# Attention quotients as small reciprocals copied out by ScalarE, gate products dealt out thinner, and two of four low parts on VectorE, in a two-layer diffusion trunk

## The chip, the core and the metric

The kernel runs on one core of a Trainium2 chip. A core has five engines with a queue of instructions each: TensorE (PE: matrix products and transposes; weight loads are shown as PEld), VectorE (DVE), ScalarE (ACT), GpSimd (POOL) and SyncE (SP, which here only issues DMA transfers). Each engine works through its queue in order and waits on semaphores for what other engines and transfers have to deliver. The metric is the device time of one execution in microseconds (us); lower is better.

## The reference

Two layers of a trunk with two attention branches side by side. 512 latent tokens on an 8 x 64 grid and 256 context tokens; model width 1024; branches A and B have 8 query heads of 64 each.

```python
for l in range(DEPTH):                       # 2 layers
    hx = rmsnorm(x) * (1 + scale_x) + shift_x      # scale, shift, gate = silu(c) @ w_ada + b_ada
    a_k, a_v, b_k, b_v, a_q, b_q, a_z, b_z, g_a, g_b = split(hx @ w_in)
    a_att = neighbourhood attention (8 x 16 window, position bias, QK-norm) plus all context keys
    qb = rope_2d(rmsnorm(b_q)); kb = rope_2d(rmsnorm(b_k))
    b_att = softmax(qb . k_all / 8) @ v_all        # 2 key/value heads, 768 keys
    o_a = (a_att * silu(a_z)) @ w_o_a
    o_b = (b_att * silu(b_z)) @ w_o_b
    merged = sigmoid(g_a) * o_a + sigmoid(g_b) * o_b
    x = x + gate_x * (merged @ w_out)              # context tokens likewise, in layer 0 only
```

All inputs and the output are fp32.

## The kernel before, in words

**Precision.** An fp32 product is made of three products of a faster format: each operand is split into a high part (a rounded copy) and a low part (the rest), and high x high, low x high and high x low are summed (lines 423 to 425). So each weight tile `raw` that is loaded needs a cast by ScalarE (`whi`, L393 or L408) and a subtraction by VectorE or GpSimd (`wlo`, L396 or L410). Softmax weights are turned by DMA: ScalarE casts `p` to fp16 (`h`, L824), VectorE or GpSimd subtracts for the low part (L825), and a DMA transpose (L829, issued by SyncE) writes `ht`.

**Stages of a layer.** Projections and the neighbourhood attention of branch A; the projection of branch B's keys and values; then the stages that the change touches:

- *Branch B's queries.* `for t in range(qt): tok_proj(w_q, 512, a_hx, t, evac_bq)` runs one tile of 128 tokens after the other (six in layer 0, four in layer 1). Per tile the evacuation squares on ScalarE, sums on VectorE (L493), takes the power on GpSimd (L496), multiplies on VectorE (L505), applies the rotary or, for context tokens, the norm weight (`rr`, L574, L579), and TensorE transposes `rr` some pieces later (L517).
- *Gate products.* In layer 0 the list `bg` holds what the adaptive gate still needs: two loads of the conditioning vector and 32 dot products on VectorE (L285), two for each 128x512 tile `rawb` of w_ada that SyncE loads into one of two buffers. Twelve items run in the key/value projection, 22 are left for the query projection, `run(bg, 4)` after each tile. In layer 1 the list is empty there.
- *Fill pieces.* Products that the attention doesn't depend on (gate columns of w_in, then the output projection of branch A, `o_chunks("a", ...)`) are cut into pieces; `PRE_GQ * len(spans)` of them (four in layer 0) run ahead of the attention, the others between its blocks. Their accumulator `psf` is one PSUM buffer, emptied by ScalarE (L612) or, for branch A's output, by VectorE (`tg`, L694).
- *Grouped-query attention.* Eight blocks u. `gq_first(u)`: four times scores on TensorE (L879, L880) into one of two PSUM buffers `pss`, the maximum on VectorE (L1151), the exponential on ScalarE (L1152), which frees `pss` and adds up the row sums `r`, then the transposition as above. `gq_second(u)`: `divide`, then the products with the values (`pair_values`, L844) and the multiplication into `zb` (L1179). `divide` (L831 to L837) takes the 128x4 sums of a block, repeats each 64 times, takes the reciprocal of the 128x256 result on VectorE (L834), turns it by two TensorE transposes (L836) and multiplies it into the gate `zb` (L837). There are 20 divisions: eight blocks in each layer, and four for context queries in layer 0 (sums `rc`).
- *`prepare`*, a fill piece: splits the gated output of branch A, `za`, into `gah` (four casts by ScalarE, L658) and `gal` (four subtractions by GpSimd, L659), and issues the first two of four gate loads `tg` (1.5 MB each in layer 0).

**What sets the order.** The kernel is written in a tile framework whose scheduler gives each engine its order of instructions from a timeline of its own; a few orders are tied by hand (`behind`). So an edit in one place moves rows in many others.

Of the kernel before, what the change touches and what calls it, by code (L numbers as in the profile page):

```python
# [12 lines left out]
ALU = mybir.AluOpType  # L13
# [38 lines left out]
def R(ap):  # L52
    return ap.bitcast(F32R)
# [7 lines left out]
def hybrid_kernel(es: ExitStack, tc, x, ctx, cvec, w_ada, w_ada0, small, gvec, w_in, w_o_a, w_o_b, w_out,  # L61
# [521 lines left out]
    def layer(l, hx, nxt, start):  # L583
        first = l == 0
        ntok = NTOK if first else NLAT
# [67 lines left out]

        def hilo(src, dst, fs, lo_eng=G, parts=((0, ntok),)):
            sv = src.rearrange("p (f n) -> p f n", f=4)
            for n0, n1 in parts:
                for f in fs:
                    S.copy(R(dst[0][:, f, n0:n1]), sv[:, f, n0:n1])  # L658
                    lo_eng.tensor_tensor(R(dst[1][:, f, n0:n1]), sv[:, f, n0:n1], dst[0][:, f, n0:n1], ALU.subtract)  # L659

# [20 lines left out]
        def prepare():  # L681

            gated["a"] = hilo_tiles("ga")
            hilo(za, gated["a"], range(4))
            for c in (0, 2):
                tg[c] = big("tg")
                load_tg(c)
# [90 lines left out]
        if True:  # L778
# [52 lines left out]
            def divide(ps, r, dst, back):  # L831

                rb = att["p"].tile([128, 2, 128], F32, tag="rb", name=nm("rb"), bufs=2)
                V.reciprocal(rb.rearrange("p i (e d) -> p i e d", e=2), r.unsqueeze(3).to_broadcast([128, 2, 2, 64]))  # L834
                for i in range(2):
                    T.transpose(ps[:, 128 * i:128 * i + 128], rb[:, i, :], ident)  # L836
                V.scalar_tensor_tensor(dst, ps, back, dst, ALU.mult, ALU.mult)  # L837
# [274 lines left out]
            for t in range(qt):  # L1112
                tok_proj(w_q, 512, a_hx, t, evac_bq)
                run(bg, 4)
                if t == STAGE_T[0]:
                    split_vb()
                if t in STAGE_T:
                    e = STAGE_T.index(t)
                    stage_k(kbv[:, 0, :], e, gkt[e][0], gkt[e][1], True)

            zb = big("zb")
            for i in range(PRE_GQ * len(spans)):
                run(fill, 1)
                turn_late(1 if i == 0 else 0)
            bp_es.close()
            gq_es = open_att(f"gq{l}", 768, NP_GQ[l], 0, NH_GQ[l])
# [64 lines left out]
        with tc.tile_pool(name=f"mrg{l}", bufs=1, reuse_waits="tile") as mp:  # L1191
# [3 lines left out]
            for v in range(nv):  # L1195
                src = gd[l][8 * v:8 * v + 8].rearrange("k p -> (k p)").unsqueeze(0)
                nc.sync.dma_start(gv[:, v, :], src.to_broadcast([128, DM]))
            hilo(zb, gated["b"], [3], V, spans)
            mg = []
# [313 lines left out]
```

## Time and profile before

| | us |
|---|---|
| three runs of the kernel | 1111.32, 1114.02, 1115.77 (median 1114.02) |
| the profiled execution | 1115.85 |
| its span, from the first instruction to the last | 1114.1 |
| TensorE busy | 1074.7 |
| VectorE, ScalarE, GpSimd busy | 783.1, 607.9, 441.2 |
| mean granted TensorE clock | 0.995 |

The profile is of one execution. Its span is the time in which instructions ran; 1.75 us of the execution's time lie around it. "Busy" counts an engine's own instructions, not its waits. A wait is put down to the instruction that released it: "PE pst L836 <- DVE rb L834: 2.2, 2, 1.4" reads: TensorE's line 836, which writes `pst`, waited for VectorE's line 834, which wrote `rb`; 2.2 us in all, 2 times, the longest 1.4. In the stretches, times count from the start of the span: 330 to 371 is the query projection of layer 0, 371 to 381 the fill pieces behind it, 381 to 540 the grouped-query attention of layer 0, 925 to 1064 that of layer 1.

### The profile page before, as it was taken

How to read it: one execution, taken by the hardware profiler on the slowest of the kernel's cores; microseconds unless marked ns; L12 is line 12 of the kernel's file. 1: busy time of each engine (PE TensorE's matmuls, PEld its weight loads, DVE VectorE, ACT ScalarE, POOL GpSimd, SP SyncE). 2: the span in 40 equal slices, each digit the busy share in tenths (PEclk: the TensorE clock that was granted, in tenths of full speed). 3: DMA queues.
4: the chain of work that ended last, by engine and by line, in shares of the span. 5: the costliest groups of instructions: out<-in, count | busy, mean ns of one | idle time of the engine just before them, and what ended most of it. 6: DMA issues, size and time to landing. Idle time of an engine off the chain costs nothing. (4 is left out here: it accounts for less than half of the span.)

```text
span 1114.1 us, 17673 instructions
## 1 busy us (share of the span) xinstructions
PE 1074.7 (96%) x6032; PEld 883.2 (79%) x6032; DVE 783.1 (70%) x1626; ACT 607.9 (55%) x1236; POOL 441.2 (40%) x375
## 2 busy tenths in 40 slices
PE   8999999899999899988999999999999999999998
PEld 5688888788887778876888778888877888877777
DVE  4667799974388486766576875466997665879573
ACT  6464279776333467665231275444999346676430
POOL 1054235554256143353412444332455472453531
PEclk9999999999999999999999999999999999999999
DMA  9455325555545277789624532453555536889742
GB/s 369 149 169 149 90 70 116 124 137 121 174 121 179 86 177 185 174 219 248 210 76 130 189 120 69 136 170 102 126 145 126 150 113 171 195 236 218 201 151 77
DMA packets 236002, 171.83 MB, mean 154 GB/s; under 512 B 160140, under 2 KB 201864, under 8 KB 234248
## 3 DMA queue, kind: packets, MB, share of 16 engines
q1 hardware_dynamic: 228576, 156.31, 51.6%
q0 software_dynamic: 2368, 7.87, 2.1%
q10 hardware_dynamic: 4968, 6.53, 1.8%
q8 instruction: 47, 0.77, 0.3%
q14 instruction: 43, 0.35, 0.1%
HBM read 115.58 MB, written 17.32 MB: 119 GB/s over the span
## 5 line engine op out<-in xcount | busy, mean ns | idle before, releaser
L825 POOL TENSOR_TENSOR h<-p,h 128x256 f16<-128x256 f32 (+2 forms) x104 | 111.2, 1078 | 199.5 <-ACT h L824 154.2
L410 POOL TENSOR_TENSOR wlo<-raw,whi 128x512 fp32r<-128x512 f32 x70 | 97.7, 1399 | 136.8 <-ACT whi L408 100.5
L423 PE MATMUL psf<-hx,whi 128*128 128x512 f32 (+1 forms) x360 | 137.3, 382 | 1.5 <-DVE zt L614 1.2
L424 PE MATMUL psf<-hx,whi 128*128 128x512 f32 (+1 forms) x360 | 135.7, 377 | 0.0
L425 PE MATMUL psf<-hx,wlo 128*128 128x512 f32 (+1 forms) x360 | 135.3, 376 | 0.0
L408 ACT CAST whi<-raw 128x512 fp32r<-128x512 f32 x136 | 82.9, 620 | 74.0 <-DMA raw<-in_w_in_dram 52.5
L423 PE MATMUL psx<-whi,hx 128*128 128x512 f32 (+1 forms) x328 | 121.7, 373 | 0.0
L424 PE MATMUL psx<-wlo,hx 128*128 128x512 f32 (+1 forms) x328 | 120.1, 367 | 1.3 <-DVE wlo L396 1.3
L425 PE MATMUL psx<-whi,hx 128*128 128x512 f32 (+1 forms) x328 | 120.1, 367 | 0.0
L396 POOL TENSOR_TENSOR wlo<-raw,whi 128x512 fp32r<-128x512 f32 x40 | 59.2, 1483 | 126.5 <-ACT whi L393 83.1
L393 ACT CAST whi<-raw 128x512 fp32r<-128x512 f32 x88 | 54.0, 624 | 94.3 <-PE psx L425 32.1
L496 POOL TENSOR_TENSOR ss<-ss,ehalf 128x8 f32<-128x8 f32 (+2 forms) x40 | 63.6, 1594 | 78.0 <-DVE ss L493 69.6
L824 ACT CAST h<-p 128x256 f16<-128x256 f32 (+2 forms) x136 | 81.2, 617 | 12.3 <-DMA ht<-h 9.3
L1151 DVE CUSTOM_DVE_ANT_0 p<-pss,vb 128x768 f32<-128x768 f32 x64 | 59.9, 949 | 35.1 <-PE pss L880 31.2
L1152 ACT ACTIVATE p<-pss,mx 128x768 f32<-128x768 f32 x64 | 57.5, 901 | 41.0 <-DVE mx L1151 40.6
L423 PEld LDWEIGHTS psf<-hx,whi 128*128 128x128 f32 x360 | 67.8, 188 | 14.7 <-DVE zt L614 1.6
L410 DVE TENSOR_TENSOR wlo<-raw,whi 128x512 fp32r<-128x512 f32 x66 | 60.8, 925 | 26.3 <-ACT whi L408 26.2
L425 PEld LDWEIGHTS psf<-hx,wlo 128*128 128x128 f32 x360 | 67.8, 188 | 11.7
L424 PEld LDWEIGHTS psf<-hx,whi 128*128 128x128 f32 x360 | 67.9, 189 | 11.2 <-issue 0.6
L424 PEld LDWEIGHTS psx<-wlo,hx 128*128 128x128 f32 x328 | 62.0, 189 | 11.6 <-DVE wlo L396 2.4
L425 PEld LDWEIGHTS psx<-whi,hx 128*128 128x128 f32 x328 | 61.9, 189 | 10.5 <-DVE hx L339 0.4
L423 PEld LDWEIGHTS psx<-whi,hx 128*128 128x128 f32 x328 | 61.9, 189 | 9.4 <-issue 0.2
(330 smaller groups left out, 2938.9 us busy)
## 6 DMA issues: line engine op xcount, KB each, us to landing
raw<-in_w_in_dram SPq DMA_DIRECT2D x168, 256.0 KB, 3.0
rawb<-in_w_ada_dram SPq DMA_DIRECT2D x48, 256.0 KB, 2.7
raw<-in_w_out_dram SPq DMA_DIRECT2D x32, 256.0 KB, 2.9
tg<-gs SPq DMA_DIRECT2D x4, 1536.0 KB, 8.4
rawx<-in_w_ada_dram SPq DMA_DIRECT2D x4, 1024.0 KB, 10.2
rawy<-in_w_ada_dram SPq DMA_DIRECT2D x4, 1024.0 KB, 9.9
gs<-zt ACTq DMA_DIRECT2D x16, 256.0 KB, 2.6
raw<-in_w_o_a_dram SPq DMA_DIRECT2D x16, 256.0 KB, 3.7
```

Source lines behind the costliest of these rows:

```text
L393: S.copy(hi[:, :n], raw[:, :n])
L396: e.tensor_tensor(lo[:, :n], raw[:, :n], F(hi[:, :n]), ALU.subtract)
L408: S.copy(hi, raw)
L410: lo_eng(i).tensor_tensor(lo, raw, F(hi), ALU.subtract)
L423: T.matmul(ps, lhs[0], rhs[0], start=first, stop=False)
L424: T.matmul(ps, lhs[0], rhs[1], start=False, stop=False)
L425: T.matmul(ps, lhs[1], rhs[0], start=False, stop=last)
L496: G.tensor_tensor(ss, ss, ehalf[:, :n], ALU.pow)
L824: S.copy(h[:, 0], p[:, :n])
L825: eng.tensor_tensor(h[:, 1], p[:, :n], h[:, 0], ALU.subtract)
L1151: V.tensor_tensor_reduce(p, pss, lift, -1.0, 3e38, ALU.add, ALU.min, mx[:, 0:1])
L1152: S.activation(p, pss, AF.Exp, bias=mx[:, 0:1], accum_out=r[:, i, e:e + 1])
```

## The change

Three edits.

1. `divide` takes the reciprocal of the 128x4 sums in place on VectorE, and ScalarE then writes each of them 64 times side by side into `rb`.
2. After each tile of the query projection three items of `bg` run where four did, and after each of the four fill pieces one more; whatever is then left runs at once.
3. `hilo` takes a tuple of engines and goes round it: `gal` 0 and 2 on VectorE, 1 and 3 on GpSimd, in both layers. The other calls keep their engine.

```diff
-        def hilo(src, dst, fs, lo_eng=G, parts=((0, ntok),)):
+        def hilo(src, dst, fs, lo_eng=(G,), parts=((0, ntok),)):
...
-                    lo_eng.tensor_tensor(R(dst[1][:, f, n0:n1]), sv[:, f, n0:n1], dst[0][:, f, n0:n1], ALU.subtract)
+                    lo_eng[f % len(lo_eng)].tensor_tensor(R(dst[1][:, f, n0:n1]), sv[:, f, n0:n1], dst[0][:, f, n0:n1], ALU.subtract)
...
-            hilo(za, gated["a"], range(4))
+            hilo(za, gated["a"], range(4), (V, G))
...
-                V.reciprocal(rb.rearrange("p i (e d) -> p i e d", e=2), r.unsqueeze(3).to_broadcast([128, 2, 2, 64]))
+                V.reciprocal(r, r)
+                S.copy(rb.rearrange("p i (e d) -> p i e d", e=2), r.unsqueeze(3).to_broadcast([128, 2, 2, 64]))
...
             for t in range(qt):
                 tok_proj(w_q, 512, a_hx, t, evac_bq)
-                run(bg, 4)
+                run(bg, 3)
...
             for i in range(PRE_GQ * len(spans)):
                 run(fill, 1)
                 turn_late(1 if i == 0 else 0)
+                run(bg, 1)
+            run(bg, len(bg))
...
-            hilo(zb, gated["b"], [3], V, spans)
+            hilo(zb, gated["b"], [3], (V,), spans)
```

Lines behind the edits move: L836 becomes L837, L837 L838, L844 L845, L879 L880, and from the second edit on by three (L1151 becomes L1154, L1152 L1155, L1179 L1182).

VectorE's order at the end of layer 0's query projection, from the first context tile's `rr` (L574) to the second's, which is the last tile's. `junk` and `rawb` as outputs are dot products (L285; their second rows, of the sums, are left out), `wlo` a low part, `ss` the norm's sums. Before:

```order
594 L574 TENSOR_TENSOR rr_4048<-ry_4046,gbc_3413 128x512
595 L410 TENSOR_TENSOR wlo_3796<-raw_3792,whi_3794 128x512
596 L285 ISA rawb_4012,asum<-rawb_4012,cb_3888 128x512
598 L493 TENSOR_REDUCE ss_815_4091<-sq_3407 128x8
599 L285 ISA junk_4058,asum<-rawb_4056,cb_3888 128x512
601 L285 ISA rawb_4056,asum<-rawb_4056,cb_3888 128x512
603 L285 ISA junk_4063,asum<-rawb_4061,cb_3888 128x512
605 L505 TENSOR_TENSOR ry_4095<-psx_4066,ss_815_4091 128x512
606 L285 ISA rawb_4061,asum<-rawb_4061,cb_3888 128x512
608 L574 TENSOR_TENSOR rr_4097<-ry_4095,gbc_3413 128x512
```

With the change:

```order
587 L505 TENSOR_TENSOR ry_4036<-psx_4007,ss_802_4032 128x512
588 L574 TENSOR_TENSOR rr_4038<-ry_4036,gbc_3413 128x512
589 L410 TENSOR_TENSOR wlo_3796<-raw_3792,whi_3794 128x512
590 L285 ISA junk_4048,asum<-rawb_4046,cb_3888 128x512
592 L493 TENSOR_REDUCE ss_811_4080<-sq_3407 128x8
593 L285 ISA rawb_4046,asum<-rawb_4046,cb_3888 128x512
595 L285 ISA junk_4053,asum<-rawb_4051,cb_3888 128x512
597 L505 TENSOR_TENSOR ry_4084<-psx_4055,ss_811_4080 128x512
598 L574 TENSOR_TENSOR rr_4086<-ry_4084,gbc_3413 128x512
599 L285 ISA rawb_4051,asum<-rawb_4051,cb_3888 128x512
```

Between the two L574 there were five dot products and are three now; seven follow the last L574 where two did.

VectorE around `prepare` in layer 0 (`p` with `mx` is a score's maximum, the first `zb` of a pair L837 or L838 the quotient times the gate). Before:

```order
752 L1179 TENSOR_TENSOR zb_4110<-pst_5539,zb_4110 128x256
753 L834 RECIPROCAL rb_5731<-r_1068_5468 128x256
754 L834 RECIPROCAL rb_5773<-rc_5312 128x256
755 L1151 ISA p_5663,mx_5664<-pss_5658,vb_3419 128x768
757 L1151 ISA p_5676,mx_5677<-pss_5671,vb_3419 128x768
759 L837 SCALAR_TENSOR_TENSOR zb_4110<-pst_5729,vb_3419,zb_4110 128x256
760 L837 SCALAR_TENSOR_TENSOR zb_4110<-psv_5730,vb_3419,zb_4110 128x256
```

With the change:

```order
747 L834 RECIPROCAL r_1068_5474<-r_1068_5474 128x4
...
753 L1182 TENSOR_TENSOR zb_4100<-pst_5545,zb_4100 128x256
754 L1154 ISA p_5670,mx_5671<-pss_5665,vb_3419 128x768
756 L838 SCALAR_TENSOR_TENSOR zb_4100<-pst_5736,vb_3419,zb_4100 128x256
757 L834 RECIPROCAL rc_5316<-rc_5316 128x4
758 L659 TENSOR_TENSOR gal_5412<-za_1053,gah_5411 128x768 x2
759 L1154 ISA p_5683,mx_5684<-pss_5678,vb_3419 128x768
764 L838 SCALAR_TENSOR_TENSOR zb_4100<-psv_5737,vb_3419,zb_4100 128x256
```

Two reciprocals in a row stood ahead of the next block's first maximum; now two low parts stand between its first and second.

ScalarE in the last block of layer 0 with the change (L1155 exponentials, L902 those of the context, L835 the new copies):

```order
547 L1155 ACTIVATE p_5894,r_1145_5875<-pss_5889,mx_5895 128x768
548 L1155 ACTIVATE p_5907,r_1145_5875<-pss_5902,mx_5908 128x768
549 L1155 ACTIVATE p_5920,r_1145_5875<-pss_5915,mx_5921 128x768
550 L408 CAST whi_6154<-raw_6152 128x512
551 L835 COPY rb_6074<-r_1145_5875 128x256
552 L824 CAST h_5898<-p_5894 128x768
553 L658 CAST gbh_6064<-zb_4100 128x768 x3
```

The copy comes right behind the block's last exponential and one cast, ahead of three casts `h` that the transposes need.

SyncE at `prepare` in layer 0 (`tg` gate loads, `ht` and `vb` transposes). Before:

```order
232 L662 DMA tg_5415<-gs_83 128x3072
233 L662 DMA tg_5417<-gs_85 128x3072
234 L829 DMA_TRANSPOSE ht_5467<-h_5517 128x12x128
235 L829 DMA_TRANSPOSE vb_3419<-h_5535 128x8x128
236 L829 DMA_TRANSPOSE ht_5656<-h_5667 128x12x128
237 L405 DMA raw_5811<-in_w_o_a_dram 128x2x256
238 L662 DMA tg_6050<-gs_84 128x3072
239 L662 DMA tg_6052<-gs_86 128x3072
```

With the change:

```order
232 L829 DMA_TRANSPOSE ht_5473<-h_5523 128x12x128
233 L662 DMA tg_5421<-gs_83 128x3072
234 L662 DMA tg_5423<-gs_85 128x3072
235 L662 DMA tg_6060<-gs_84 128x3072
236 L829 DMA_TRANSPOSE vb_3419<-h_5541 128x8x128
237 L405 DMA raw_5820<-in_w_o_a_dram 128x2x256
238 L829 DMA_TRANSPOSE ht_5663<-h_5674 128x12x128
```

The third gate load has moved up behind the first two, ahead of the context's transpose and of the next block's first; the fourth now stands alone, three transposes later.

## The prediction

> **What bounds the kernel now.** I read the page's head first: whichever engine fills the span sets the time.
>
> ```profile
> span 1114.1 us, 17673 instructions
> PE 1074.7 (96%) x6032; PEld 883.2 (79%) x6032; DVE 783.1 (70%) x1626; ACT 607.9 (55%) x1236; POOL 441.2 (40%) x375
> ```
>
> TensorE is busy for 1074.7 of 1114.1 us. The change takes no matmul away, so all that it can win is TensorE's idle time (39 us in the whole program) and time at a halved clock. Next come the stretches that it touches, as busy time by engine (PE, PEld, DVE, ACT, POOL, then granted clock, DMA share, GB/s): the last projection of branch B in layer 0, the fill pieces behind it, the grouped-query attention of layer 0 in two parts, and that of layer 1 in two parts.
>
> ```profile
> 330.00:371.00 41.00, 36.71 (x177) 29.97 (x176) 35.65 (x76) 14.14 (x27) 22.00 (x13) 0.96 0.43 145
> 371.00:381.00 10.00, 10.00 (x57) 8.71 (x57) 0.90 (x3) 3.86 (x7) 1.29 (x1) 1.00 0.20 66
> 381.00:484.00 103.00, 100.52 (x692) 83.92 (x691) 75.31 (x131) 69.14 (x146) 33.98 (x23) 1.00 0.73 169
> 484.00:540.00 56.00, 48.70 (x340) 38.48 (x339) 35.45 (x59) 29.55 (x57) 28.47 (x20) 0.97 1.01 259
> 925.00:990.00 65.00, 63.89 (x375) 52.59 (x373) 47.20 (x71) 46.00 (x86) 26.09 (x17) 1.00 0.74 177
> 990.00:1064.00 74.00, 69.90 (x435) 54.95 (x434) 57.28 (x82) 42.35 (x76) 34.60 (x24) 1.00 0.88 224
> ```
>
> TensorE idles 4.3, 0, 2.5, 7.3, 1.1 and 4.1 us there, 19 us in all. What it waits for, in the last projection (2 rows), then in layer 0's attention (7), then in layer 1's (6):
>
> ```profile
> PE pst L517 <- DVE rr L574: 3.2, 1, 3.2
> PE pst L517 <- DVE rr L579: 1.0, 1, 1.0
> ...
> PE pst L836 <- DVE rb L834: 2.2, 2, 1.4
> PE pst L844 <- DVE zb L837: 1.7, 1, 1.7
> PE psf L424 <- POOL gal L659: 1.5, 1, 1.5
> PE psf L423 <- DVE tg L694: 1.5, 4, 0.5
> PE pss L879 <- ACT p L1152: 1.2, 3, 0.7
> PE pss L879 <- ACT p L901: 0.7, 1, 0.7
> PE pst L844 <- DMA ht<-h: 0.7, 1, 0.7
> ...
> PE pss L879 <- ACT p L1152: 2.3, 3, 1.5
> PE psf L423 <- DVE tg L694: 1.2, 3, 0.6
> PE pst L836 <- DVE rb L834: 0.8, 1, 0.8
> PE psf L423 <- ACT zt L612: 0.3, 1, 0.3
> PE psf L424 <- POOL gal L659: 0.3, 1, 0.3
> PE psf L423 <- ACT gbh L658: 0.3, 1, 0.3
> ```
>
> Nearly all of them are on VectorE, or on ScalarE behind a maximum of VectorE.
>
> **Part 1, the spread dot products.** The timeline at the end of the last projection:
>
> ```profile
> 364.59 0.69 DVE L285 CUSTOM_DVE_ANT_0 junk<-rawb,cb 128x512 bf16<-128x512 f32 x1 [1.68 <-DMA rawb<-in_w_ada_dram]
> 365.21 0.69 DVE L505 TENSOR_TENSOR ry<-psx,ss 128x512 f32<-128x512 f32 x1
> 366.42 0.69 DVE L574 TENSOR_TENSOR rr<-ry,gbc 128x512 f32<-128x512 f32 x1
> 382.12 0.96 DVE L1151 CUSTOM_DVE_ANT_0 p<-pss,vb 128x768 f32<-128x768 f32 x1 [10.16 <-PE pss L880]
> 367.25 1.08 PE L517 MATMUL pst<-ident,rr 128*128 128x128 f32 x4 [3.25 <-DVE rr L574]
> 369.41 0.63 PE L424 MATMUL psx<-hx,whi 128*128 128x512 f32 x1
> 370.35 0.40 PE L424 MATMUL psx<-hx,whi 128*128 128x512 f32 x1
> ...
> 367.00:370.00 3.00, 2.75 (x9) 2.39 (x10) 2.62 (x10) 1.58 (x4) 0.00 (x0) 0.51 0.00 0
> ```
>
> A dot product that waits 1.68 us for its weight tile stands in VectorE's line ahead of the last tile's L505 and L574, and the transposes of that tile wait 3.25 us. The windows' row at the bottom gives half clock for the 3 us after (0.63 us for a matmul that takes 0.40 once it is over): 1.5 us of lost rate, of which I count 1.3, since its first 0.25 is the stall's own. In the new order L505 and L574 stand ahead of two of these products, one load's wait sooner, and the tile before goes two products earlier. The 3.25 and the 1.3 go if L574 ends before about 364.0, where TensorE asks for it; one dot on a new load stays ahead of it, so I leave 0.5 us of wait. The 1.05 for L579, whose engine was busy with dots too, goes as well. Gain 3.25 + 1.05 + 1.3 - 0.5 = **5.1**. The five dots that move past L574, 0.69 us each, 3.5 in all, land in VectorE's pause of 10.16 us before the first maximum; TensorE runs fill pieces there with VectorE busy 0.90 of 10. Their loads move on SyncE's queue as well, ahead of the fill's fourth weight load; without that cover the first scores would wait the 3.5. Bounds: 0 (the loads hold L505 as before) to 5.6.
>
> The Trainium skill ("TensorE: Matmul & The Clock Gate", Part 1: The HAM clock gate) has the clock halved after an idle window of about 3.4 us. The 3.25 us stall and the row at 0.51 agree; by that rule the 1.3 goes with the stall, as I count it, but the second halved stretch below, behind waits of 1.40 us at most, would not be tied to one stall.
>
> **Part 2, the reciprocals.** The groups, and two small stand-ins that the kernel already has:
>
> ```profile
> L834 DVE RECIPROCAL rb<-r 128x256 f32<-128x256 f32 x16 | 28.0, 1748 | 1.0 <-ACT p L1152 0.8
> L834 DVE RECIPROCAL rb<-rc 128x256 f32<-128x256 f32 x4 | 6.9, 1723 | 0.3 <-ACT p L901 0.3
> L781 DVE RECIPROCAL r<-r 128x2 f32<-128x2 f32 x8 | 1.3, 157 | 1.5 <-ACT p L901 1.5
> L824 ACT CAST h<-p 128x256 f16<-128x256 f32 x64 | 24.1, 401 | 2.1 <-DVE p L787 1.0 <-issue 0.5
> ```
>
> VectorE gives up 28.0 + 6.9 = 34.9 us and takes on 20 x 0.157 = 3.1; ScalarE takes on 20 x 0.40 = 8.0, priced by a copy of the same width. A copy from a stride of zero is in no row: the bounds are 0.40 and the 1.75 of the reciprocal that read so, and I take 0.40, since the reciprocal's price fits its arithmetic. From a quotient that is ready to the transposes it is 0.16 + 0.40, some 0.7 with a handover between engines (an estimate), in place of 1.75: each wait on rb shrinks by about 1.0. So of 2.2 us in layer 0 (0.8 and 1.4) I take 1.8, in layer 1 all 0.8. The 1.7 for zb stands behind two reciprocals in a row; but two low parts now stand at that place (part 3), so half of it: 0.8. Of the waits for tg and for L1152 (2.7 and 3.5 us), which end when VectorE comes to an L694 or a maximum, I take a third with less in the line: 0.5 and 0.4 in layer 0, 0.4 and 0.8 in layer 1.
>
> The copy is also a new wait. ScalarE's order puts it behind the block's last exponentials, and each copy waits for VectorE's small reciprocal with casts and the next block's exponentials queued behind; those free the two score buffers for TensorE. I charge 1.5 us for it; bounds 0 (ScalarE is busy 53 to 71% in these stretches) and the rival below.
>
> **Part 3, the low parts of gal.**
>
> ```profile
> L659 POOL TENSOR_TENSOR gal<-za,gah 128x768 fp32r<-128x768 f32 x4 | 7.9, 2015 | 0.0
> L659 POOL TENSOR_TENSOR gal<-za,gah 128x512 fp32r<-128x512 f32 x4 | 5.5, 1397 | 0.0
> 518.67 0.95 DVE L825 TENSOR_TENSOR h<-p,h 128x768 f16<-128x768 f32 x1
> 539.25 3.93 DVE L659 TENSOR_TENSOR gbl<-zb,gbh 128x512 fp32r<-128x512 f32 x2
> ```
>
> Two of four leave GpSimd, so the chain of 7.9 us ends about 4 us sooner and the waits on it (1.5 and 0.3) go. On VectorE the like is 0.95 us alone, but 1.97 each for two smaller ones beside GpSimd's own; I take 2.0, so 4.0 us in one block, against 3.4 us of two reciprocals that stood there. Between 1.9 and 5: no net term.
>
> The Trainium skill ("SBUF — State Buffer", SBUF: two separate sides) says that GpSimd and a VectorE instruction with two SBUF inputs hold the shared port in turn, the loser blocked for the whole instruction. The row 539.25 looks like it. Taken whole, it makes the pair cost VectorE the 4.0 that I use.
>
> **The second half of layer 0's attention** needs a brake. DMA share is 1.01 over 484 to 540 (above): four gate loads of 1.5 MB share the queues with the transposes of h. And there is a second halved stretch:
>
> ```profile
> 527.00:530.00 3.00, 3.00 (x9) 2.11 (x7) 1.87 (x2) 1.28 (x4) 3.00 (x3) 0.50 1.21 271
> ```
>
> Where transfers set the pace, a VectorE that is ready sooner waits for them. Layer 0's candidates are 1.8 (rb) + 0.8 (zb) + 1.5 (gal) + 0.5 (tg) + 0.4 (L1152) = 5.0, and 0.7 for half of this stretch's loss: 5.7. I take half, **2.9**. Layer 1's are 0.8 (rb) + 0.3 (gal) + 0.4 + 0.8 = 2.3, with DMA at 0.74 to 0.88; I take **2.0**.
>
> **The sum.** 5.1 + 2.9 + 2.0 - 1.5 = 8.5 us from the profiled execution's 1115.85 (span 1114.1 and 1.75 around it) gives 1107.35. That execution lies at the top of the three runs, 1.8 above their median of 1114.02, so the median comes to 1105.5: **1105**, rounded down. A scheduler orders all instructions anew, past the attention too; I put that at 0, with 3 us either way.
>
> **The rivals.**
>
> *Transfers set the pace* in both second halves (DMA 1.01 and 0.88, a third gate load now stands directly behind the first two on SyncE, ahead of two transposes that it followed before). For it: the same row's share. Against: of 9.5 us waited in layer 0 only 0.7 is put down to a DMA. Then the projection gains 5.1, the two early rb waits about 0.8 each, less 1.5 for the copies: 5.2, or 1114.0 - 5.2 = 1109.
>
> *ScalarE's line is the new bound* (slower). A copy reaches the head before VectorE has come to its small reciprocal, which stands behind low parts (0.95 to 2.0 us) and a maximum (0.96): up to 3 us in which the next exponentials stand still. Speaking for it: L1152 already holds scores back 3.5 us. Against: a wait costs TensorE only once both score buffers are full, and a block has 17 to 20 us (139 and 159 us for 8 of them). At 1.0 us of TensorE for each of 20 copies, 20 less the gains of 5.1 + 2.9 + 2.0 makes 10 us lost: 1124. It is slower than before from 0.5 us each.
>
> *The projection's stall stays* because GpSimd's power and the load, not the dots, end last: 1.0 of 5.1 is won, the rest as forecast: 1114.0 - 4.4 = 1109.6.
>
> **Chances.** Forecast (1100 to 1108) 0.58; transfers 0.18; stall stays 0.12; ScalarE's line 0.07; something better than the forecast, with the halved stretch and the whole of the waits gone (up to 19 us of idle), 0.05. The range 1099 to 1114 leaves out the slower rival and the best case and takes in the bounds between; the likeliest case alone is 1100 to 1108. What differs by less than 0.5% (5.6 us) can hardly be told from no change: faster is below 1108.4, which holds the forecast, the best case and few of the others: 0.64. Slower is above 1119.6: 0.07. Same: 0.29.
>
> **What would show it.** Right: no wait on rr at L517 above 0.5 us and clock 1.00 around 367; VectorE's busy time down by about 32 less 7 for the low parts; the new copies at 0.40; no wait on gal. Wrong: the copies at over 1 us, more waiting on L1155 (L1152 before) than 3.5 us, TensorE waiting for qs or pss at the first scores because dots run late, or as much idle time in 484 to 540 with DMA in the place of VectorE.

## The result, and the profile after

The changed kernel takes 1097.99 us (median of four runs, 1095.73 to 1103.31) where the kernel before takes 1113.88: 0.9864 of it, 95% interval 0.9835 to 0.9892. Measured a second time it gave 0.9863 (0.9841 to 0.9884). That is 14 to 16 us faster, and the time lies below the predicted range, which began at 1099. The direction was right; nearly half of the gain was not foreseen.

The page's head after:

```profile
span 1095.5 us, 17697 instructions
PE 1066.4 (97%) x6032; PEld 882.3 (81%) x6032; DVE 757.7 (69%) x1630; ACT 613.6 (56%) x1256; POOL 438.5 (40%) x371
```

The same 6032 matmuls fill 8.3 us less, for the most part because fewer of them ran at half clock (the mean granted clock is 1.000 in place of 0.995, which is worth 5.6 us), and TensorE idles 29.1 us in place of 39.4. The stretches that answer to those of the prediction (query projection, fill pieces, layer 0's attention in two parts, layer 1's in two; columns as there):

```profile
330.00:367.00 37.00, 33.72 (x170) 27.67 (x169) 30.76 (x60) 12.06 (x21) 20.95 (x13) 1.00 0.50 150
367.00:378.00 11.00, 11.00 (x62) 9.57 (x61) 5.76 (x19) 3.96 (x9) 1.38 (x1) 1.00 0.29 94
378.00:475.00 97.00, 95.24 (x662) 80.86 (x661) 63.72 (x126) 70.91 (x150) 36.35 (x24) 1.00 0.74 174
475.00:529.00 54.00, 50.93 (x373) 42.08 (x372) 31.28 (x67) 32.30 (x64) 25.15 (x18) 1.00 0.99 271
914.00:975.00 61.00, 60.44 (x360) 49.80 (x359) 39.35 (x68) 46.55 (x87) 26.07 (x17) 1.00 0.78 187
975.00:1046.00 71.00, 69.24 (x439) 55.20 (x438) 48.20 (x84) 44.13 (x80) 33.84 (x22) 1.00 0.90 229
```

The clock is 1.00 in all of them: both halved stretches are gone. In the second half of layer 0's attention TensorE idles 3.1 us in place of 7.3, although the DMA share is 0.99 as before. TensorE's waits in the query projection (2 rows), layer 0's attention (6) and layer 1's (5):

```profile
PE pst L517 <- DVE rr L579: 1.8, 1, 1.8
PE pst L517 <- DVE rr L574: 1.5, 1, 1.5
...
PE pst L845 <- DVE zb L838: 1.4, 1, 1.4
PE psf L423 <- DVE tg L694: 1.1, 2, 1.0
PE psv L845 <- DMA vb<-h: 0.8, 1, 0.8
PE pst L837 <- ACT rb L835: 0.8, 2, 0.6
PE pst L845 <- DMA ht<-h: 0.3, 1, 0.3
PE psv L837 <- ACT rb L835: 0.2, 1, 0.2
...
PE pss L880 <- ACT p L1155: 0.8, 2, 0.5
PE psf L423 <- ACT gbh L658: 0.7, 1, 0.7
PE psf L423 <- ACT zt L612: 0.4, 1, 0.4
PE pst L837 <- ACT rb L835: 0.2, 1, 0.2
PE pst L845 <- DMA ht<-h: 0.2, 1, 0.2
```

In the two attentions 9.5 and 5.2 us have become 4.6 and 2.3. The waits on gal are gone, those on rb are 1.2 where they were 3.0, and scores wait 0.8 us for exponentials (L1155) where it was 3.5. The durations, on VectorE, GpSimd and ScalarE:

```profile
L834 DVE RECIPROCAL r<-r 128x4 f32<-128x4 f32 x16 | 2.8, 175 | 3.9 <-ACT p L1155 3.8
L659 DVE TENSOR_TENSOR gal<-za,gah 128x768 fp32r<-128x768 f32 x2 | 3.4, 1683 | 0.1
...
L659 POOL TENSOR_TENSOR gal<-za,gah 128x768 fp32r<-128x768 f32 x2 | 4.8, 2418 | 4.9 <-ACT gah L658 4.9
...
L835 ACT COPY rb<-r 128x256 f32<-128x256 f32 x16 | 6.4, 403 | 0.5 <-DVE r L834 0.5
```

The prices were close: 0.17 us for the small reciprocal (0.16 forecast), 0.40 for the copy (0.40), 1.7 for a low part on VectorE beside GpSimd (2.0; it is the mean of 0.96 and 2.41). VectorE is busy 25.4 us less, 25 were forecast.

**Where the time went.** For each matmul I take the time until the next one starts, less the least that its shape takes (its tenth percentile in the profile before), and add these up: idle time and slow clock together, in us. The change was profiled twice.

```
                                              before   change   change again
start, up to branch B's first transposes        49.7     48.5     49.7
query projection and fill pieces, layer 0        9.9      7.6      7.9
grouped-query attention, layer 0                45.4     36.8     38.0
merge behind it, layer 0                         4.5      6.4      6.5
turn from layer 0 to layer 1                     9.5      6.4      6.4
layer 1, up to its grouped-query attention      22.1     21.3     21.5
grouped-query attention, layer 1                30.2     25.3     27.4
from there to the end                            3.2      3.6      3.6
sum                                            174.5    155.9    161.0
```

The second row begins in the key/value projection, some 25 us ahead of the queries' first transposes. An attention is counted up to its last product with the values; the merge is what follows it, up to the last product of layer 0's output projection. So the query projection gave 2.2 us (mean of both), layer 0's attention 8.0, of which the merge behind it lost 2.0 again, layer 1's attention 3.9, and 3.1 came from a place that no edit touches: the turn, from that last product (about 650 us before) to the transposition of layer 1's gate sums (760).

### The profile page after: what moved, and what is told of

It reads as the page before. It is cut to its first block, busy times and chain, and to the rows that moved or that the text cites. A ratio compares the mean times of both kernels' runs of the same rounds, so it can differ in the third digit from the quotient of the medians.

```text
span 1095.5 us, 17697 instructions
## 1 busy us (share of the span) xinstructions
PE 1066.4 (97%) x6032; PEld 882.3 (81%) x6032; DVE 757.7 (69%) x1630; ACT 613.6 (56%) x1256; POOL 438.5 (40%) x371
## 5 line engine op out<-in xcount | busy, mean ns | idle before, releaser
L825 POOL TENSOR_TENSOR h<-p,h 128x256 f16<-128x256 f32 (+2 forms) x104 | 113.8, 1102 | 192.1 <-ACT h L824 141.5
L396 POOL TENSOR_TENSOR wlo<-raw,whi 128x512 fp32r<-128x512 f32 x40 | 60.1, 1507 | 123.7 <-ACT whi L393 69.9
L1154 DVE CUSTOM_DVE_ANT_0 p<-pss,vb 128x768 f32<-128x768 f32 x64 | 60.3, 954 | 31.0 <-PE pss L881 27.5
L410 DVE TENSOR_TENSOR wlo<-raw,whi 128x512 fp32r<-128x512 f32 x66 | 63.4, 963 | 23.6 <-ACT whi L408 23.3
L1155 ACT ACTIVATE p<-pss,mx 128x768 f32<-128x768 f32 x64 | 57.6, 901 | 25.5 <-DVE mx L1154 25.1
```

What stands on the lines that cost most here:

```text
L396: e.tensor_tensor(lo[:, :n], raw[:, :n], F(hi[:, :n]), ALU.subtract)
L410: lo_eng(i).tensor_tensor(lo, raw, F(hi), ALU.subtract)
L825: eng.tensor_tensor(h[:, 1], p[:, :n], h[:, 0], ALU.subtract)
L1154: V.tensor_tensor_reduce(p, pss, lift, -1.0, 3e38, ALU.add, ALU.min, mx[:, 0:1])
L1155: S.activation(p, pss, AF.Exp, bias=mx[:, 0:1], accum_out=r[:, i, e:e + 1])
```

## The experiments

All ratios are to the kernel before, with 95% intervals, each from runs beside the kernel before on one chip; the tables set ratios from three chips side by side. "Beyond work" is the measure of the table above, in the same stretches. It comes from one profile of each kernel: the change's own two profiles differ by 1.2 us in layer 0's attention and by 2.1 in layer 1's, so a difference of that size in one stretch says little.

### Each part alone

The edits are the three of the change, one at a time on the kernel before, and the quotients in layer 1 alone (`if first:` the old reciprocal, `else:` the new pair).

> The kernel before with the quotients alone changed (small reciprocal on VectorE, copy by ScalarE). Theory 1, VectorE's 32 us less set the pace in both attentions even though transfers are dense there: 10 to 12 us faster (about 1102 to 1104), with the attention of layer 0 about 6 us shorter and that of layer 1 about 4. Theory 2, what was forecast, transfers hold half of it back: 2 to 3 us faster (about 1111). Theory 3, much of the whole change's 16 us is a lucky new order of instructions outside the attentions: 4 to 6 us, and the stretch from layer 0's merge to layer 1's first attention moves by several us in this run or in one of the other parts.

> The kernel before with the dot products alone spread out. By the forecast's step 5.1 us faster (about 1109); by the trace of the whole change, where TensorE still waits 1.8 us for the rotary result of one tile and 1.5 us for that of the last, 2.5 us (about 1111.5). Theory 3 (new orders): anything from -3 to +3 beside that, with its place outside the query projection.

> The kernel before with two of the four low parts of branch A's gated output on VectorE alone. Forecast's step: the 1.5 and 0.3 us waits on GpSimd's chain go, VectorE is blocked 4 us longer beside two reciprocals that are still there: 0 to 2 us faster (about 1112.5 to 1114). Theory that VectorE sets the pace: 0 to 2 us slower, since 7.4 us of reciprocals and low parts now stand in one block ahead of the maxima. Theory 3: up to 3 us either way from places elsewhere.

> The kernel before with the new quotients in layer 1 alone; layer 0 as before. Theory 1: the attention of layer 1 is about 4 us shorter and nothing else moves (about 1109.5). Theory 2 (transfers): 1 to 2 us. Theory 3: the stretch from layer 0's merge to layer 1's first attention also moves by a few us although nothing in it was edited.

```
                                                               layer 0                  layer 1
                         ratio (interval)            query  attention  merge  turn  attention  to the end
before                                                 9.9     45.4     4.5    9.5     30.2       3.2
quotients                0.9954 (0.9940 to 0.9968)    11.5     39.5     3.9   15.1     28.5       0.7
dot products             0.9978 (0.9961 to 0.9994)     8.1     45.7     4.4    9.5     30.2       3.1
low parts of gal         0.9980 (0.9966 to 0.9993)    11.0     43.0     2.8   12.6     30.8       0.6
quotients in layer 1     0.9965 (0.9952 to 0.9977)    11.5     44.7     4.6    9.4     29.7       0.7
```

Alone the parts win 5.1, 2.5 and 2.2 us, 10 together, not 15. The columns say why. The quotients win 5.9 us in layer 0's attention and lose 5.6 at the turn; the low parts win 2.4 there and lose 3.1 at the turn. With layer 0 unedited, the turn stands at 9.4. The two gains in layer 0's attention add up to about what the whole change won in it (8.0). There theory 1 (VectorE's time sets the pace) holds with its 6 us, and theory 2 (transfers keep half of it) does not.

In layer 1's attention theory 1 expected 4 us, and the quotients won 1.7 there, or 0.5 when they are in layer 1 alone. TensorE's longest waits in it are now for transposes by DMA, for which it did not wait there before. With the quotients alone:

```profile
PE pst L845 <- DMA ht<-h: 2.3, 3, 0.8
```

So theory 1 does not hold there. Nor does theory 2 for the most part: two of these three transposes took some 4 us, not far from the usual (median 3.5), and were issued within 0.7 us of GpSimd's low part of `h` (L825), so it is that chain which is late; only the third, 7.5 us long, was slow itself. What these two runs won behind it, 2.5 us in "to the end", stands where nothing was edited: a wait of 1.7 us for a low part of a weight tile by GpSimd (L396) in layer 1's output projection is gone. So theory 3 is right that a stretch without an edit moves by several us.

What TensorE waits for at the turn, with the quotients alone:

```profile
PE pst L331 <- ACT half L334: 2.2, 2, 1.5
PE psx L424 <- POOL wlo L396: 1.9, 2, 1.3
```

VectorE's timeline there: the last dot product of the second modulation, and the row that makes layer 1's scale and shift (`modc`, L230):

```profile
644.11 0.69 DVE L285 CUSTOM_DVE_ANT_0 rawb<-rawb,cb 128x512 f32<-128x512 f32 x1
645.37 0.17 DVE L230 TENSOR_TENSOR modc<-modc,g 128x16 f32<-128x16 f32 x1
```

The window behind them:

```profile
649.00:660.00 11.00, 9.15 (x32) 6.62 (x31) 8.28 (x11) 9.29 (x23) 7.28 (x7) 0.69 0.37 103
```

With the whole change, the same two rows of the timeline:

```profile
628.68 0.68 DVE L285 CUSTOM_DVE_ANT_0 rawb<-rawb,cb 128x512 f32<-128x512 f32 x1
631.07 0.17 DVE L230 TENSOR_TENSOR modc<-modc,g 128x16 f32<-128x16 f32 x1
```

and the window at the same place of the program, with no wait of TensorE in it:

```profile
638.00:649.00 11.00, 11.00 (x58) 9.16 (x57) 10.38 (x16) 10.03 (x25) 6.26 (x7) 1.00 0.31 96
```

L334 applies layer 1's scale and shift to the transposed tokens. It can't begin before L230, which ends a chain of 16 weight loads (issued by GpSimd, two buffers) and 32 dot products on VectorE. From its first dot product to the start of L230 the chain lasts 47 to 48 us in all three kernels: 596.8 to 644.3 before, 598.1 to 645.4 with the quotients alone, 582.7 to 631.1 with the change. The output projection's last product starts at 650.3, 644.8 and 640.2. So the quotients bring TensorE to the turn 5.5 us sooner and the chain 1.1 us later; TensorE stands, and then runs at a clock of 0.69. With the change the chain begins 14 us sooner.

### Half of the chain left out

On the kernel before, on the quotients alone and on the whole change, the same edit. It leaves out 8 of the 16 loads and 16 of the 32 dot products, so layer 1's scale and shift lack their part:

```diff
-            bg = ada_steps(1, range(16), (1,), 2, mp, G) + [lambda: ada_mod(1)] if first else []
+            bg = [lambda: V.memset(asum[:, 8:16, 1, 0:2], 0.0)] + ada_steps(1, range(8), (1,), 2, mp, G) + [lambda: ada_mod(1)] if first else []
```

> The changed kernel once more, beside the next three on one chip: 0.986 of before again (about 15 us faster). If the three parts simply added up (5.1 + 2.5 + 2.2 us, as each alone gave) it would be 10 us faster, 0.991.

> The kernel before, with half of the second modulation's dot products in layer 0's merge left out (8 of 16 weight tiles, their sums set to zero, so layer 1's scale and shift are not the reference's). New theory: TensorE's stalls at the turn from layer 0 to layer 1 (9.4 us beyond its work in the kernel before, 15.1 with the quotients alone, 6.4 with the whole change) come from the modulation, whose chain of loads and dot products takes some 47 us from where the scheduler starts it. Then half of the chain takes the turn to about 6 us: 3 us faster than before. Rival: the stalls come from casts and low parts at the turn: within 1 us of before.

> The quotients alone, with the same half of the modulation left out (layer 1's scale and shift are not the reference's). New theory: the 5 to 6 us that the quotients win in layer 0's attention and lose again at the turn stay won: some 8 us faster than the quotients alone (about 13 us below before). Rival, casts and low parts: within 1 to 2 us of the quotients alone (5 us below before).

> The whole change, with the same half of the modulation left out (layer 1's scale and shift are not the reference's). New theory: the chain already ends in time there, so nothing is won: within 1.5 us of the whole change. Rival, that less work for VectorE in the merge helps anyway (16 products, some 12 us of VectorE): 2 us or more faster.

```
                             ratio (interval)            turn    in the whole chain's kernel
change again                 0.9863 (0.9841 to 0.9884)    6.4
before, half chain           0.9961 (0.9946 to 0.9977)    6.1     9.5 (ratio 1)
quotients, half chain        0.9895 (0.9876 to 0.9914)    5.7    15.1 (0.9954)
change, half chain           0.9842 (0.9827 to 0.9857)    6.1     6.4 (0.9863)
```

The turn falls to 6 us in all three, from 9.5, 15.1 and 6.4. The total follows less neatly: 4.4, 6.6 and 2.3 us faster (3, 8 and at most 1.5 were expected) where 3.4, 9.4 and 0.3 come from the turn; the rest lies elsewhere. Casts and low parts stayed as they were, so that rival falls. For the whole change the other rival's figure came, 2 us or more by less work for VectorE, but the intervals overlap and nothing of it shows at the turn.

### The chain begun early, nothing left out

Leaving work out could help by the work. So the chain was only moved: its list is made ahead of the merge's first chunk, and four items run after each of the four chunks.

```diff
+            bg = ada_steps(1, range(16), (1,), 2, mp, G) + [lambda: ada_mod(1)] if first else []
+            run(bg, 1)
             chunks = o_chunks("b", None, evac_b)
...
                 for piece in chunks[i][1]:
                     piece()
+                run(bg, 4)
```

> The quotients alone, with the second modulation's loads and dot products begun in the merge's first products (four after each chunk of weights), nothing left out. Theory of the late chain: the turn falls from 15 to about 6 us beyond TensorE's work and the total to about 0.988 (8 us faster than the quotients alone). Rival, that the missing work of the half-chain runs and not its time made the difference: no gain, or a loss, since VectorE now has 16 products more in the merge.

> The whole change with the modulation's chain begun early, nothing left out. By the theory of the late chain nothing is to be won here, as the chain is already early enough with the change (6.4 us at the turn, as where half of it was left out): 0.986 within 0.002. Rival, that an early chain helps by itself: 2 to 3 us faster, 0.984.

With the quotients alone the turn falls from 15.1 to 8.2 us and the total from 0.9954 to 0.9918 (0.9894 to 0.9943): 4 us faster with the same work, half of what was expected. The merge, into which the dot products moved, took 6.5 us beyond work and not 3.9, which fits the rival's loss, beside the gain. With the whole change the turn goes from 6.4 to 6.1, the merge from 6.4 to 8.1, and the total is 0.9885 (0.9865 to 0.9904): no faster than 0.9863, as expected, though just outside the 0.002 that I gave. Over all kernels the turn goes with one number, the start of the chain's last row (L230) less the start of the output projection's last product:

```
                                        chain's last row less last product   turn
quotients / copy on VectorE / low parts       +0.5 / +0.3 / -0.2        15.1 / 13.1 / 12.6
before / dots / quotients in layer 1          -6.0                       9.5 /  9.5 /  9.4
change (twice) / engines swapped              -9.0                       6.4
begun early, or half left out                -14 to -25                  8.2 to 5.7
```

A late chain is shown as the cause of the turn's part: in six kernels it was shortened or begun early, and the turn fell in each, by most where the chain had been latest. It isn't the whole of it: with the quotients alone and the chain begun early, 14 us ahead, the turn is 8.2 and not 6.4, and TensorE waits 1.3 us for low parts of weight tiles (L396) there. That the whole change begins the chain early is the scheduler's order.

### Which part brings the early order

Quotients and low parts without the dot products; and the whole change with the engines of gal swapped, `(G, V)` for `(V, G)`.

> Quotients and low parts without the spread dot products. If the attentions' gains add up: 5 to 6 us in layer 0's, 3 to 4 in layer 1's. The turn between the layers is open: with the modulation's chain late as with the quotients alone (15 us beyond TensorE's work) the total is near 0.992; with it early as in the whole change (6 us) near 0.988, and then the low parts, not the dots, bring the early order.

> The whole change with the two engines of the low parts swapped (0 and 2 on GpSimd, 1 and 3 on VectorE): the same work, so what moves is the order alone. If the scheduler's order at the turn is a matter of luck: the attentions within 1 to 2 us of the whole change's, the turn anywhere from 6 to 15 us beyond TensorE's work, the total anywhere from 0.986 to 0.994. If not: 0.986 again, with 6 us at the turn.

Quotients and low parts together: 0.9903 (0.9875 to 0.9932), turn 6.4. So these two bring the early chain, where each alone made it late. Layer 0's attention wins 6.2 us (39.2 in place of 45.4; 5 to 6 were expected), layer 1's 2.9 (3 to 4), but the merge takes 7.9 us beyond work, against 6.4 and 6.5 with the dot products. In the attention and the merge behind it stand two half-clock stretches that the change's profiles don't have:

```profile
527.70:531.10 3.40, 3.40 (x10) 2.61 (x9) 0.00 (x0) 0.00 (x0) 0.00 (x0) 0.50 0.91 216
544.80:548.20 3.40, 3.40 (x15) 3.30 (x16) 0.42 (x1) 0.00 (x0) 0.00 (x0) 0.50 0.39 148
```

They cost 3.4 us, about as much as the two stretches together take more. This profile is also of the slowest of the kernel's six runs (1109.60 us, median 1105.19), so how much of the difference is the order's is open. Swapped: 0.9871 (0.9850 to 0.9892), turn 6.4, attention 37.2, merge 5.9. So this swap leaves the chain where it was. Not every small edit does: the copy on VectorE and two dot products per tile, both below, move it back.

### VectorE's time, ScalarE's line, the transfers

The copy by VectorE in the whole change:

```diff
-                S.copy(rb.rearrange("p i (e d) -> p i e d", e=2), r.unsqueeze(3).to_broadcast([128, 2, 2, 64]))
+                V.tensor_copy(rb.rearrange("p i (e d) -> p i e d", e=2), r.unsqueeze(3).to_broadcast([128, 2, 2, 64]))
```

> The whole change, but the copy side by side on VectorE in place of ScalarE. Theory A, what counts is VectorE's time: 0.16 us and a copy of about 0.4 against 1.75 still free it of 1.2 us for each division, three quarters of what the change frees; both attentions stay within 2 us of the whole change's, 0.986 to 0.989 of before. Theory B, the forecast's charge of 1.5 us for waits in ScalarE's line is real: the attentions get 1 to 2 us shorter than with the change. A shift at the turn between the layers is read apart, by the time beyond TensorE's work there.

0.9938 (0.9922 to 0.9954). Its groups, 16 copies for latent queries and 4 for context:

```profile
L835 DVE COPY rb<-r 128x256 f32<-128x256 f32 x16 | 9.5, 595 | 0.5
L835 DVE COPY rb<-rc 128x256 f32<-128x256 f32 x4 | 1.6, 402 | 0.1
```

Layer 0's attention took 40.0 us beyond work, against 36.8 and 38.0 with ScalarE; its merge only 1.9, against 6.4 and 6.5; layer 1's attention 28.6, against 25.3 and 27.4; the turn 13.1, with the chain 0.3 us late. So ridding VectorE of the 1.75 us gives most of the gain in layer 0's attention (5.4 of 8.0 us), the copy by ScalarE some 2 to 3 us more, and of the 8 us between the totals 6.7 lie at the turn again. Theory A's total (0.986 to 0.989) did not come, for the turn's sake above all. Theory B does not hold: without the copies in ScalarE's line the attentions are longer, not shorter. TensorE's longest waits in layer 0's attention:

```profile
PE pst L845 <- DVE zb L838: 3.8, 2, 2.5
PE pst L845 <- DMA ht<-h: 3.2, 2, 2.9
```

The copy itself took 0.29 to 0.30 us in 13 of the 20 cases, and 0.46 to 1.63 in the other seven, in all of which GpSimd was at an instruction of its own (see the last section).

Each gate load issued twice in the whole change (`load_tg` with its line twice):

> The whole change with each of the eight gate loads issued twice (6.3 MB more in layer 0's second half of the attention, 4.2 MB in layer 1's). Rival of the forecast, transfers set the pace there: at some 200 to 260 GB/s that is 20 us or more of queue, of which at least 8 us show in the total. Theory that VectorE and what hangs on it set the pace, and transfers have room: within 2 us of the whole change.

1.0046 (1.0028 to 1.0063): 20 us slower than the change. Layer 0's attention took 50.7 us beyond work, 13 to 14 more than with the change; layer 1's 33.2, 6 to 8 more. TensorE's waits in layer 0's attention:

```profile
PE pss L881 <- ACT p L1156: 4.7, 2, 3.5
PE psf L423 <- DVE tg L695: 3.1, 4, 1.7
PE pst L846 <- DMA ht<-h: 2.8, 2, 2.2
PE pst L846 <- DVE zb L839: 2.6, 2, 1.4
PE psv L846 <- DMA vb<-h: 2.3, 1, 2.3
```

So 10.5 MB more cost far more than nothing: my theory that the transfers have room falls, and the rival's "at least 8 us" came. How much of it is the transfers' own time is not shown. Only 5.1 of these 15.5 us are put down to a DMA, the second loads also moved SyncE's other issues, and TensorE's clock was halved for 13.7 us of the stretch. Nor does it say that transfers set the pace with the loads as they are: there the waits on DMA are 1.1 us in layer 0 (rows above), and the attention got shorter by 8 us at the same DMA share. With the copy on VectorE TensorE did wait 2.9 us for one transpose in layer 0 that took 11.3 us, where the median is 3.8. So they stand close to it.

### The rest of the query projection, and a faster version

Two dot products per tile and three per fill piece (`run(bg, 2)`, `run(bg, 3)`), then the same with the early chain, then with gbl's three low parts on VectorE too (`hilo(zb, gated["b"], range(3), (V,))`), then with all four of gal as well (`(V,)`):

> The whole change with two dot products after each tile of the query projection and three after each fill piece (3 and 1 in the change). TensorE still waits 1.8 and 1.5 us for rotary results with the change. If dots ahead of them are the cause: 1 to 3 us faster than the whole change, in the stretch of the query projection. Against it: ten products on five loads then run behind the projection, some 13 us, up to the first maximum: 0 to 3 us slower by late first scores.

> Two dot products per tile in the query projection and three per fill piece, with the modulation's chain begun early as in the run before. The 3 us that the former won in the query projection and lost at the turn should stay won: turn 9.5 to about 6, total 0.984 (2 to 3 us faster than the change). Rival: the same as the change, 0.987.

> The same, and the three low parts of branch B's gated output that GpSimd does (1.85 us each, beside which VectorE's two take 3.5 us each in place of 0.7) on VectorE as well. If the two engines block each other there, all on VectorE is 3 x 0.95 + 2 x 0.7 = 4.3 us in place of 7.0, and TensorE's wait of 2.1 us for tg behind them goes: 1 to 2 us faster than without. Rival: VectorE is fuller and the next block's maxima wait: 0 to 2 us slower.

> The version with two dots per tile, the early chain and all low parts of branch B on VectorE, with branch A's four low parts on VectorE too. VectorE at 0.95 us each takes 3.8 us in one block, as long as two beside GpSimd's two: within 1 us of the former version (0.9826). Rival: the maxima queue behind four: 1 to 3 us slower.

```
                                                               layer 0
                            ratio (interval)            query  attention  merge  turn
two dots per tile           0.9873 (0.9854 to 0.9891)    4.1     41.1      4.9    9.5
and the early chain         0.9835 (0.9810 to 0.9861)    4.2     41.6      5.6    6.5
and gbl on VectorE          0.9826 (0.9799 to 0.9853)    4.1     40.9      5.6    6.5
and gal on VectorE          0.9861 (0.9844 to 0.9878)    4.1     43.3      7.6    6.1
```

Two dots per tile take the query projection from 7.6 to 4.1 us beyond work; no wait for rr is left. The total stays, as the turn goes back to 9.5 and the attention to 41.1, where a half-clock stretch of 6.8 us stands. With the early chain the turn's 3 us come back. The third version, 1095.36 us as a median, is the fastest found: 20 us below before, and some 4 below the change by the ratios. The intervals of the two overlap, so that it beats the change is likely, not certain; against the second version its 1 us can't be told from none. All of gal on VectorE is 4 us slower than that, where at most 1 was expected. Those intervals overlap too, so this speaks for the split of the change and does not prove it.

## Why the prediction was right or wrong

**Part 1, the dot products: too high.** Forecast 5.1 us. The change gained 2.2 here, and alone 2.5 in the total. The step that failed is "I leave 0.5 us of wait" with the whole of L579's 1.05: 1.5 and 1.8 us remained. After the change, at the last tile:

```profile
359.76 0.69 DVE L493 TENSOR_REDUCE ss<-sq 128x8 f32<-128x520 f32 x1
362.58 0.69 DVE L505 TENSOR_TENSOR ry<-psx,ss 128x512 f32<-128x512 f32 x1 [0.91 <-POOL ss L496]
363.30 0.69 DVE L574 TENSOR_TENSOR rr<-ry,gbc 128x512 f32<-128x512 f32 x1
...
364.14 0.63 PE L517 MATMUL pst<-ident,rr 128*128 128x128 f32 x4 [1.51 <-DVE rr L574]
```

I had L505 freed from the load, and it was; but L505 now waits for GpSimd's power, whose sum (L493) still stood behind a dot product and a low part. I followed one link of the chain and not the one before it. The mechanism was right (two dots per tile remove both waits), and so was the cover for the moved dots: they end at 371.1, the first maximum begins at 378.6. The halved clock behind L574 went, as counted, but that the change's profile has none in this stretch is in part luck: in five of the eight kernels with three dots per tile it halves earlier instead, for 3.4 us from 355 to 357 on, behind the wait for L579. In the eight kernels where this stretch is unedited its time beyond work runs from 8.5 to 12.2 us, 11.0 in the mean, in the eight with three dots from 7.4 to 8.1, 7.9 in the mean. So the gain is rather 3 us than 2.2, and known to about 1 us only.

**Parts 2 and 3 in the attentions: too low.** Forecast 2.9 + 2.0 - 1.5 = 3.4 us; it was 8.0 + 3.9 = 11.9, and 9.9 with the 2.0 that the merge lost. This is where most of the miss lies.

The step that failed in layer 0 is "I take half", taken because the DMA share was 1.01. Of the 5.0 us of waits among the candidates TensorE's idle time in the attention fell by 4.3 (from 9.8 to 4.8 and 6.1), nearly the whole, with the share still 0.99. The share says that transfers are busy; the waits in the profile already said whom TensorE waits for: 9.5 us, of which 0.7 on DMA. The other 3.7 us of the 8.0 are time beyond work that isn't idle, for which I had 0.7, half of the loss at 527 to 530. That stretch's 1.5 us went whole; where the other 2 come from is open. Term by term the sum of the waits came by luck: those on rb fell by 1.2 and not 1.8, that for zb by 0.3 and not 0.8, those for exponentials by 1.9 where I took 0.4.

Next, the charge of 1.5 us for the copies. Behind exponentials, where I put it, there is none: those waits fell from 3.5 to 0.8. On the copies themselves TensorE still waits 1.2 us, where my terms for rb had left 0.4; so some 0.8 us of the charge was real, and in other orders more (2.4 us in layer 0 with the quotients alone). The copy on VectorE, which avoids it, is slower all the same.

Last, layer 1's 2.0 were 3.9: the waits for exponentials went from 2.3 to 0.8, where I took a third. With the quotients alone they fell less, to 1.7, and TensorE waited for transposes instead, most of them late by GpSimd's low part of `h`; only with all the edits did the gain come. That it is the low parts of gal, taken from GpSimd, which free these transposes would fit, but is not shown.

**The new orders: 0 forecast, 3 us either way.** The turn alone gave 3.1, and with single parts it cost up to 5.6. My bound came from no row, so that the change fell on the good side of it was luck. The rows were there: in the profile before, the chain's last row starts 6 us ahead of the projection's last product, so whatever brings TensorE there sooner without the chain comes to stand behind it.

**The median:** the step from the profiled execution to the runs (1.8 us) held for before (1113.88); the change's two profiled spans differ by 5 us themselves.

**The rivals.** That transfers set the pace (0.18) did not happen. That the stall stays (0.12) happened in part: 3.3 of 4.3 us of waits remained, by GpSimd's power and VectorE's order rather than the load, though without the halved clock behind L574. ScalarE's line (0.07) did not happen: all waits on the copies are 1.2 us. What came in number was the case "better than the forecast" (0.05). Its condition came by half: the halved stretches went, but of the 19 us of idle in these stretches 10.4 remained, and the turn's 3 us made up for part of that. With 5.7 us of candidates at hand and one reason to halve them, 0.05 was too little, and the range should have begun where the candidates come whole: 1114.0 - (5.1 + 5.7 + 2.3) = 1100.9, and 3 to 6 us below for the orders.

## What to carry to other kernels

Read whom the bounding engine waits for, and take those waits off whole where the edit removes their cause; a busy share of transfers alone is no reason to halve them. Then ask who is next in line: with the quotients alone the waits in layer 1 went over to transposes. Cut the stretches finely enough, too: an attention and the merge behind it moved in opposite directions here, and their sum hid it. Look past the edited stage for the next fixed chain (loads and dot products on a clock of their own, here 47 us): what an earlier stage wins reaches the end only if that chain starts earlier too, and measuring parts one at a time mixes their gains with where the chain happens to start. When a stall is to go, follow its chain back by two links, not by one.

## What the runs showed of the hardware

Now and then a VectorE subtraction with both operands in SBUF lasted through three GpSimd instructions, not one. After the change, at the end of layer 0's attention, VectorE, GpSimd and TensorE:

```profile
528.98 6.66 DVE L659 TENSOR_TENSOR gbl<-zb,gbh 128x512 fp32r<-128x512 f32 x2
...
529.32 5.43 POOL L659 TENSOR_TENSOR gbl<-zb,gbh 128x768 fp32r<-128x768 f32 x3
...
536.29 0.39 PE L423 MATMUL psf<-gah,whi 128*128 128x256 f32 x1 [2.15 <-DVE tg L694]
```

The two subtractions are one of 128x512, which took 6.33 us, and one of 128x256, which took 0.41 (not 3.5 each, as one expectation above has it). The same subtraction of 128x512 ran 0.69 us in layer 1, where GpSimd was idle. Here it ended 0.55 us after GpSimd's third, although it had begun 0.34 us ahead of the first, and TensorE waited 2.15 us for the row behind it: that is what the merge lost. With the low parts of gal alone changed it took 5.26 us in the same way. In the kernel before, beside the same three on GpSimd, the pair took 1.95 and 2.06 us, and the first of them ended 0.55 us after GpSimd's first. The Trainium skill ("SBUF — State Buffer", SBUF: two separate sides) has the loser blocked for the other's whole instruction; the kernel before agrees with that, while with the change the wait spans three. Which case comes is not explained by these runs. With all five low parts on VectorE the ratio was 0.9826 against 0.9835, no difference that the intervals tell apart; but the version compared had the short case (1.95 and 2.06 us), so whether this removes the long one was not tried.

A copy on VectorE with one operand in SBUF waited for GpSimd too. With the copies on VectorE:

```profile
516.57 1.63 DVE L835 COPY rb<-r 128x256 f32<-128x256 f32 x1
...
516.39 1.66 POOL L825 TENSOR_TENSOR h<-p,h 128x768 f16<-128x768 f32 x1 [2.71 <-ACT h L824]
```

In the seven of 20 cases that found GpSimd at an instruction it ended 0.15 us behind that instruction each time, after 0.46 to 1.63 us; the other 13 took 0.29 to 0.30. On ScalarE all 20 took 0.39 to 0.42 us, from a stride of zero, as much as a cast of the same size (0.40).
